# A two-layer trunk with 16 routed experts: fixed queue order in the experts, layer 1's first expert fed from on-chip rows, and the overflow branch moved

## The chip, the cores and the metric

One NeuronCore of one Trainium2 chip runs the whole program. The metric is the device time of one execution in microseconds (us).

## The reference

Two layers over 512 tokens of width 1024, batch 1, all in fp32. Each layer ends with the same grouped mixture of experts:

```python
for i in range(DEPTH):                                   # 2 layers
    z = x @ w_in                                         # mixer i: gMLP gating, or a short convolution
    tok, q = mixer(z), z[..., -512:]
    xa = memory_cross_attention(q, mem, w_kv[i])         # 256 memory rows
    o = concatenate([tok, xa]) @ w_out[i]
    x = layer_norm(ALPHA * x + o, ln1_g[i], ln1_b[i])
    scores = sigmoid(x @ router_w); sel = scores + router_b   # shared router, 16 experts
    # 1 of 4 groups by the sum of its top two, then the top two experts of that group
    for e in range(16):
        h = silu(x @ w_gate[i, e]) * (x @ w_up[i, e])    # 1024 -> 512
        f = f + combine[:, e] * (h @ w_down[i, e])       # 512 -> 1024
    x = layer_norm(ALPHA * x + f, ln2_g[i], ln2_b[i])
```

## The kernel before

**Products.** Every fp32 product is three fp32r products (`mm3`, L202 to L204): high by high, high by low, low by high. Weights come as 1 MB loads (`raw`, issued by SP, L147). ACT rounds each to its high part (L168) and DVE subtracts to get the low part (L169). Some splits of a 0.5 MB half (`split`) run their second step on POOL. Pages of 1 MB form a ring; a page comes free when the last reader is done, and with it a load may start.

**Mixer end** (`mixer_end`, `project_out`). The output projection makes columns 0 to 511 of all four row blocks first, then 512 to 1023 block by block (`oa`). After each block the rows are normalised (DVE), written to DRAM twice by POOL's queue (`x1d` to gather from, `rd` to add to), transposed (`rt`) and multiplied with the router (`lg`).

**Routing** (`route`, `entries`, `tables`, `overflow`). A chain of small DVE operations makes `oh` (token by expert, 0/1); products with `tri` and `ones_b` make each token's place in its expert's list (`pos`). `sel` blocks (128x128, 0/1) times `tok` make a table of token numbers and gates (`tab`, then `idxs` and `gates`); `cnt` and `nover` say whether an expert has more than 128 tokens.

**Experts** (`experts`). 16 experts, each on 128 slots: POOL gathers the rows of `x1d` into `xg`; PE transposes them (`xt`, 8 operations), ACT and DVE split them (`xgt`); PE does gate and up (`ga`, `ua`, 48 products of 512 columns), ACT Silu, DVE the product `h`, PE transposes `h` (`htr`, 4) and does down (`ya`, 24), ACT scales by the gate, POOL scatters with addition into `rd`. Expert e's down stands behind gate and up of e+1. Layer 0 fills the time until its first gather lands with keys and values of layer 1 (`fill0`: `ka`, `va`).

**Branch** (`more`, L889, L890). Every engine reads `nover` and skips a loop for overfull experts. It is skipped on these inputs, but no engine's later instructions start before it passes the branch, and it drains first. It stands behind expert 0's gate and up.

**Order.** A scheduler that simulates the program sets each engine's order, which is fixed in the program; only the tail after the last expert is written by hand.

Of the kernel before, what the change touches and what calls it, by code (L numbers as in the profile page):

```python
# [27 lines left out]
P = 128  # L28
# [7 lines left out]
E = 16  # L36
# [11 lines left out]
def trunk(ctx, tc, x, mem, w_in_a, sgu_ln_g, sgu_ln_b, sgu_w, sgu_b, w_in_b, conv_w, w_kv, w_out,  # L48
# [270 lines left out]
    def keys_values():  # L319
# [15 lines left out]
        for j in range(4):  # L335
            g = W.next()
            for kk in range(2):
                k = 2 * j + kk
                for m in range(2):
                    ms = slice(m * P, (m + 1) * P)  # L340
                    mm3(a[m], (memh[:, k, ms], meml[:, k, ms]), (g[:, 0, kk, :], g[:, 1, kk, :]),
                        k == 0, k == KB - 1)
            W.done(g)
        for m in range(2):
            split_to(vt[:, 0, m, :], vt[:, 1, m, :], a[m])
        return kt, vt
# [107 lines left out]
    def norm(r, stats, g, b, nd):  # L454
# [7 lines left out]
        vec.scalar_tensor_tensor(r, r, mv[:, 0:1], g, op0=OP.subtract, op1=OP.mult)  # L462
        rs = small.tile([P, 1], FT, name="rstd")
        vec.reciprocal(rs, sd)
        return vec.scalar_tensor_tensor(r, r, rs, b, op0=OP.mult, op1=OP.add)

    def project_out(i, ch, cl, lnp, after):
# [25 lines left out]
        for c in range(NC):  # L493
            o = acc("oa")
            for j in range(KB):
                mm3(o, lhs(order[j], c), (gs[j // 2][:, 0, j % 2, :], gs[j // 2][:, 1, j % 2, :]), j == 0, j == KB - 1)
                if c == NC - 1 and j % 2:
                    W.done(gs[j // 2])
            half(c, 1, o)
            if c % 2:  # L500
                drop(ch[c // 2], cl[c // 2])
            after(c, norm(xrow[c], st[c], lnp[:, 0], lnp[:, 1], D))
# [10 lines left out]
    def logits(c, i, lg):  # L513

        pool_e.dma_start(x1d[i][c * P:(c + 1) * P, :], xrow[c])
        pool_e.dma_start(rd[i][c * P:(c + 1) * P, :], xrow[c])
        xt = page("x1t", [P, KB, P])
        for q in range(2):
# [3 lines left out]
            act.activation(xt[:, 4 * q:4 * q + 4], t, AF.Copy)  # L522
        for k in range(KB):
# [3 lines left out]
    def route(c0, n, lg, after, rp):  # L527

        cs = slice(c0, c0 + n)

        at = [1280 if c0 else 0]

        def T(name, *shape):
            k = math.prod(shape)
            at[0] += k
            t = rp[:, at[0] - k:at[0]]
# [3 lines left out]
        def ranks(v, g, name):  # L540
# [4 lines left out]
            df, eq = T("df" + name, g, 4, 4), T("eq" + name, g, 4, 4)  # L545
# [5 lines left out]
            rk = T("rk" + name, g, 4)  # L551
# [3 lines left out]
        sc = T("sc", n, E)  # L555
        act.activation(sc, lg, AF.Sigmoid)
        sel = T("sel", n, E)
        with tc.issue_after(after.ins):
            vec.tensor_tensor(sel, sc, rb[:, None, :].to_broadcast([P, n, E]), op=OP.add)
        g4 = lambda a: a.rearrange("p n (g b) -> p (n g) b", g=G)  # L560
        rk = ranks(g4(sel), n * G, "e")
        top = T("top", n * G, 4)
        vec.scalar_tensor_tensor(top, rk, 2.0, g4(sel), op0=OP.is_lt, op1=OP.mult)
        gs = T("gs", n, G)
        vec.tensor_reduce(gs.rearrange("p n g -> p (n g)"), top, axis=AX.X, op=OP.add)
        gr = ranks(gs, n, "g").rearrange("p n g -> p (n g)")
        ing = T("ing", n * G)
        vec.tensor_scalar(ing, gr, 0.0, None, op0=OP.is_equal)
        ib = ing[:, :, None].to_broadcast([P, n * G, 4])
        vec.scalar_tensor_tensor(g4(oh[:, cs]), rk, 2.0, ib, op0=OP.is_lt, op1=OP.mult)  # L570
        oh2 = T("oh2", 2, n, E)
        for k in range(2):
            vec.scalar_tensor_tensor(g4(oh2[:, k]), rk, float(k), ib, op0=OP.is_equal, op1=OP.mult)
        entry = lambda j: tok[:, cs, :, :, j].rearrange("p c k e -> p k c e")
        vec.tensor_tensor(entry(0), oh2, row1[:, None, cs, None].to_broadcast([P, 2, n, E]), op=OP.mult)
        pos = bank([P, n, E], "pos")
        for c in range(c0, c0 + n):
            for j in range(c):
                pe.matmul(pos[:, c - c0], ones_b, oh[:, j], start=(j == 0), stop=False)
            pe.matmul(pos[:, c - c0], tri, oh[:, c], start=(c == 0), stop=True)  # L580
        os = T("os", n, E)
        vec.tensor_tensor(os, oh[:, cs], sc, op=OP.mult)
        vec.scalar_tensor_tensor(posp[:, cs, :], pos, 1.0, oh[:, cs], op0=OP.add, op1=OP.mult)
        pk = T("pk", 2, n, E)
        vec.tensor_tensor(pk, oh2, posp[:, None, cs, :].to_broadcast([P, 2, n, E]), op=OP.mult)
        vec.tensor_reduce(pos2[:, :, cs], pk, axis=AX.X, op=OP.add)
        den = T("den", n)
        vec.tensor_reduce(den, os, axis=AX.X, op=OP.add)
        rec = T("rec", n)
        vec.reciprocal(rec, den)  # L590
        vec.scalar_tensor_tensor(os, os, 1.0 / ALPHA, rec[:, :, None].to_broadcast([P, n, E]), op0=OP.mult, op1=OP.mult)
        gk = T("gk", 2, n, E)
        vec.tensor_tensor(gk, oh2, os[:, None].to_broadcast([P, 2, n, E]), op=OP.mult)
        vec.tensor_copy(entry(1), gk)
        vec.tensor_tensor(entry(2), gk, entry(1), op=OP.subtract)
        entries(range(c0, c0 + n))

    def overflow():

        cnt = tiny(E, "cnt")  # L600
# [10 lines left out]
    tab, last_entry = [], []  # L611
# [8 lines left out]
    def entries(cs):  # L620

        for c in cs:
            if c == 0:
                tab[:] = [tiny(3 * E, "tab")]
            for k in range(2):
                m = pe.matmul(tab[0], choose(pos2[:, k, c:c + 1]), tok[:, c, k].rearrange("p e t -> p (e t)"),
                              start=(c + k == 0), stop=(c + k == NC))
        last_entry.append(m.ins)

    def tables():  # L630

        t = tab[0].rearrange("p (e t) -> p e t", t=3)
        vec.tensor_scalar(idxs, t[:, :, 0], 1.0, None, op0=OP.subtract)
        return vec.tensor_reduce(gates, t[:, :, 1:3], axis=AX.X, op=OP.add)
# [15 lines left out]
    def experts(i, lnp, fill, after, stop, fine=False):  # L650
# [6 lines left out]
        xt = page("xgt", [P, 2, KB, P], FR)  # L657
# [21 lines left out]
        def gate_up(e, between=None):  # L679
            a = [acc("ga"), acc("ua")]  # L680
            for half in range(2):
                if half and between is not None:
                    between()
                for u in range(2):
                    for j in range(2):
                        g = W.next()
                        for kk in range(2):
                            k = 4 * half + 2 * j + kk
                            m = mm3(a[u], (xt[:, 0, k, :], xt[:, 1, k, :]), (g[:, 0, kk, :], g[:, 1, kk, :]),
                                    k == 0, k == KB - 1)  # L690
                        W.done(g)
            act.activation(hp[:, 0, :], a[0], AF.Silu)
            vec.tensor_tensor(hp[:, 1, :], hp[:, 0, :], a[1], op=OP.mult)
# [8 lines left out]
        def down(e, evict):  # L702
            for n in range(2):
                o = acc("ya")
                for j in range(2):
                    g = W.next()
                    for kk in range(2):
                        k = 2 * j + kk
                        mm3(o, (ht[:, 0, k, :], ht[:, 1, k, :]), (g[:, 0, kk, :], g[:, 1, kk, :]), k == 0, k == 3)
                    W.done(g)  # L710
                evict(n, o)
# [267 lines left out]
    kt, vt = keys_values()  # L979
# [56 lines left out]
    W.keep = 3  # L1036

    def mixer_end(i, ch, cl, lnp):
        lg = [tiny(3 * E, "lg"), None]

        def after(c, normed):
            if c == 0:
                W.on_pool = (lambda n: n % 2 == 1) if i == 0 else (lambda n: n % 3 != 0)
                W.keep, W.ahead = (2, 3) if i == 0 else (1, 2)
                W.pump()
            if c == NC - 1:
                lg[1] = bank([P, E], "lg3")
                lg.append(normed)
            logits(c, i, lg[1] if c == NC - 1 else lg[0][:, c * E:(c + 1) * E])
# [4 lines left out]
        project_out(i, ch, cl, lnp, after)  # L1054
        drop(lnp)
        rp = page("route", [P, 2048])
        route(0, 3, lg[0].rearrange("p (n e) -> p n e", e=E), lg[2], rp)
        route(3, 1, lg[1].rearrange("p (n e) -> p n e", e=E), lg[2], rp)
        tables()
        drop(rp)  # L1060
        overflow()
        W.ahead = 4

    mixer_end(0, ch, cl, lnp)
# [5 lines left out]
    def fill0():  # L1070
        kv1.append(keys_values())
        drop(memh, meml)
    xhl = []
# [6 lines left out]
    experts(0, (ln2_g[0], ln2_b[0]), fill0, next_x, stop)  # L1080
    kt, vt = kv1[0]
# [34 lines left out]
    W.keep = 3  # L1116
# [37 lines left out]
```

## Time and profile before

| what | us |
|---|---|
| time, median of 3 runs (lowest to highest) | 1063.36 (1061.95 to 1065.77) |
| the profiled execution | 1063.26 |
| its span | 1061.6 |
| PE busy in the span | 991.3 |
| DVE busy | 780.7 |
| ACT busy | 628.6 |

Busy time of PE is not time at full speed: it includes stretches at half clock. In rows of the trace, the first column is the start in us from the span's start, the second the duration; behind the shape stands "[idle before <- what ended it]".

### The profile page before, as it was taken

Reading aid. Unit: us, or ns where it says so; the run is one execution under the profiler, and the core shown is the slowest. Engines: PE = TensorE matmul, PEld = TensorE weight load, DVE = VectorE, ACT = ScalarE, POOL = GpSimd, SP = SyncE. Lnnn points to the kernel's source line nnn. Section 1 sums busy time; section 2 is a strip of 40 time slices with the busy share of each in tenths; the row PEclk is TensorE's granted clock in tenths of the full one; section 3 lists DMA queues with packets and bytes.
Section 4 is the critical chain, followed back from the end, with each engine's and each line's share of the span. In section 5 each row is a group of like instructions: output and inputs, shape, how many; then the busy total and the mean of one; then the engine's idle time right before and its main releaser. Section 6 shows DMA issues by size and latency. Waiting matters only on the chain. (4 is left out here: it accounts for less than half of the span.)

```text
span 1061.6 us, 12769 instructions
## 1 busy us (share of the span) xinstructions
PE 991.3 (93%) x4815; PEld 812.6 (77%) x4816; DVE 780.7 (74%) x880; ACT 628.6 (59%) x682; POOL 170.8 (16%) x115
## 2 busy tenths in 40 slices
PE   8999999769999999899899999986699999998995
PEld 6788889658888887678679887875588888886873
DVE  4638667866889976788794656475789999777885
ACT  4526533446788865767653514232688888767762
POOL 0000004311222212101101000212022222221123
PEclk9999999979999999999999999986899999999998
DMA  9713358568999999999690414492499999999934
GB/s 323 274 41 119 120 198 296 181 224 287 361 371 307 396 350 330 319 319 338 175 390 26 159 51 159 148 390 74 172 362 349 371 341 376 354 356 335 333 67 157
DMA packets 102220, 273.31 MB, mean 257 GB/s; under 512 B 10442, under 2 KB 10966, under 8 KB 102152
## 3 DMA queue, kind: packets, MB, share of 16 engines
q1 hardware_dynamic: 89480, 242.84, 62.8%
q0 software_dynamic: 11808, 26.97, 9.1%
q10 hardware_dynamic: 864, 2.62, 0.7%
q8 instruction: 39, 0.64, 0.2%
q14 instruction: 29, 0.24, 0.1%
HBM read 262.22 MB, written 26.21 MB: 272 GB/s over the span
## 5 line engine op out<-in xcount | busy, mean ns | idle before, releaser
L169 DVE TENSOR_TENSOR low<-raw,high 128x2048 fp32r<-128x2048 f32 x189 | 429.8, 2290 | 90.6 <-ACT high L168 87.2
L168 ACT ACTIVATE high<-raw 128x2048 fp32r<-128x2048 f32 x189 | 358.2, 1913 | 44.8 <-PE ga L204 33.4
L168 ACT ACTIVATE split<-raw 128x1024 fp32r<-128x1024 f32 x66 | 68.5, 1058 | 76.5 <-PE za L204 26.0
L203 PE MATMUL ua<-low,xgt 128*128 128x512 f32 x248 | 97.8, 394 | 9.0 <-DVE low L169 9.0
L202 PE MATMUL ya<-high,ht 128*128 128x512 f32 x256 | 103.5, 406 | 1.3 <-ACT high L168 1.3
L203 PE MATMUL ya<-low,ht 128*128 128x512 f32 x256 | 102.3, 400 | 2.1 <-DVE low L169 2.1
L204 PE MATMUL ya<-high,ht 128*128 128x512 f32 x256 | 101.8, 398 | 0.8 <-DVE ht L208 0.7
L203 PE MATMUL ga<-low,xgt 128*128 128x512 f32 x248 | 99.9, 403 | 2.1 <-DVE low L169 1.9
L202 PE MATMUL ga<-high,xgt 128*128 128x512 f32 x248 | 100.4, 405 | 0.0
L204 PE MATMUL ga<-high,xgt 128*128 128x512 f32 x248 | 98.1, 396 | 0.0
L169 DVE TENSOR_TENSOR split<-raw,split 128x1024 fp32r<-128x1024 f32 x57 | 68.7, 1221 | 39.7 <-ACT split L168 38.9
L202 PE MATMUL ua<-high,xgt 128*128 128x512 f32 x248 | 97.4, 393 | 0.1
L204 PE MATMUL ua<-high,xgt 128*128 128x512 f32 x248 | 96.9, 391 | 0.0
L667 POOL DMA_INDIRECT xg<-x1d,idxs x32 | 49.8, 1556 | 267.6 <-PE xt L676 238.3
L169 POOL TENSOR_TENSOR split<-raw,split 128x1024 fp32r<-128x1024 f32 x9 | 21.7, 2406 | 284.8 <-DVE sto L474 148.9
L207 ACT ACTIVATE xgt<-xt 128x512 fp32r<-128x512 f32 x64 | 36.4, 592 | 50.3 <-PE ua L203 26.0
L202 PE MATMUL za<-xh,split 128*128 128x512 f32 x160 | 61.9, 393 | 2.0 <-ACT xh L207 2.0
L203 PEld LDWEIGHTS ua<-low,xgt 128*128 128x128 f32 x248 | 46.6, 188 | 21.0 <-DVE low L169 11.7
L203 PE MATMUL za<-xl,split 128*128 128x512 f32 x160 | 62.5, 391 | 0.0
L204 PE MATMUL za<-xh,split 128*128 128x512 f32 x160 | 61.5, 390 | 0.0
L203 PEld LDWEIGHTS ya<-low,ht 128*128 128x128 f32 x256 | 48.6, 190 | 13.7 <-DVE low L169 3.1
L202 PEld LDWEIGHTS ya<-high,ht 128*128 128x128 f32 x256 | 48.6, 190 | 12.9 <-ACT high L168 1.8
(250 smaller groups left out, 1899.1 us busy)
## 6 DMA issues: line engine op xcount, KB each, us to landing
raw<-in_w_gate_dram SPq DMA_DIRECT2D x64, 1024.0 KB, 8.8
raw<-in_w_up_dram SPq DMA_DIRECT2D x64, 1024.0 KB, 8.3
raw<-in_w_down_dram SPq DMA_DIRECT2D x64, 1024.0 KB, 9.5
raw<-in_w_kv_dram SPq DMA_DIRECT2D x8, 1024.0 KB, 7.0
raw<-in_w_out_dram SPq DMA_DIRECT2D x8, 1024.0 KB, 6.1
raw<-in_w_in_b_dram SPq DMA_DIRECT2D x8, 1024.0 KB, 10.2
raw<-in_w_in_a_dram SPq DMA_DIRECT2D x6, 1024.0 KB, 5.5
x1d<-x POOLq DMA_DIRECT2D x8, 512.0 KB, 5.8
```

The costliest lines, as they stand in the source:

```text
L168: act.activation(high, src, AF.Copy)
L169: (pool_e if self.on_pool(self.count) else vec).tensor_tensor(low, src, high, op=OP.subtract)
L202: pe.matmul(o, a[0], b[0], start=start, stop=False)
L203: pe.matmul(o, a[0], b[1], start=False, stop=False)
L204: return pe.matmul(o, a[1], b[0], start=False, stop=stop)
L207: r = act.activation(hi, src, AF.Copy)
L667: pool_e.indirect_dma_start(out=xg[:, e % 2], out_offset=None, in_=x1d[i], in_offset=bass.IndirectOffsetOnAxis(ap=tabs[e][0], axis=0), bou ...
```

## The change

In both layers the experts' instructions on PE, ACT and DVE are put in the order in which the code lists them (the scheduler no longer chooses), up to expert 14. Per expert that is: gate and up of e, the next expert's transposes, down of e-1, the transposes of `h`. The product `h` and the scaling are issued ahead of the release of the last weights.

Layer 0: the list of token numbers is made and gathered from before the gates are worked out; `xg` is zeroed by ACT and not by POOL; the branch stands ahead of expert 0, behind `va`.

Layer 1: the mixer's end is written out by hand. Chunks 0 and 1 are routed between the projection's products. The first expert's rows don't come through DRAM: 0/1 blocks `sel0` times `xrow` give its transposed rows in PSUM (`rows0`, printed as `x`), fp32 products of 128 columns. The lists, gates and gathers of the other experts follow during expert 0. The branch stands behind gate and up of expert 2.

```diff
     def experts(...):
-        xg = page("xg", [P, 2, D])
-        pool_e.memset(xg, 0.0)
...
-        gather(0)
-        gather(1)
-        if i:
-            with tc.issue_after(last_entry[-1]):
-                keep_warm(8)
-        fill()
-        rest = page("more", [P, 4, FE])
-        W.keep, W.flight = 0, 4
+        begin(gather, (1, 2) if i else (0, 1))
+        end = fill()
+        if not i:
+            more(i, hy)
+        W.keep, W.flight = i, 4
...
-        xtrans(0)
-        gather(2)
+        if not i:
+            with tc.issue_after(end):
+                xtrans(0)
+            gather(2)
+        in_order()
         for e in range(E):
+            if e == last:
+                order.close()
             up = gate_up(e, ...)
+            if i and e == 2:
+                order.close()
+                rest = page("more", [P, 4, FE])
+                more(i, rest)
+                drop(rest)
+                W.keep = 0
+                in_order()
             if e + 1 < E:
                 xtrans(e + 1)
             if e + 3 < E:
                 gather(e + 3)
-            if e == 0:
-                more(i, rest)
-                drop(rest)
-                W.pump()
...
+    def mixer_end_dense(ch, cl, lnp):
+        W.keep, W.ahead = 7, 4
...
+        def first_rows(c, ks=range(KB)):
+            for k in ks:
+                k0 = 4 * P * (k // 4) + 2 * P * (k % 4 // 2) + k % 2
+                pe.matmul(rows0[k // 4][:, k % 4 * P:(k % 4 + 1) * P], xrow[c][:, k0:k0 + 2 * P - 1:2], sel0[:, c],
+                          start=(c == 0 and k % 4 == 0), stop=(c == NC - 1), skip_group_check=True)
+        with tc.manual_schedule(engines={ET.PE, ET.Activation, ET.DVE}):
...
+            o = column(3, (3, 7), part)
+            rows(3, o, False)
+            keep_rows(3, 1)
+            rows0 = [acc("x0") for _ in range(2)]
+            xts[2] = row_blocks(2)
+            first_rows(0)
...
+            route.choose(3, 1, None, third)
+            first_rows(2)
+            route.place(3, 1, route.count(3, 1))
+            choose_first(3)
+            first_rows(3)
+            xt, xg = slots()
...
+                split_to(xt[:, 0, 4 * q:4 * q + 4, :], xt[:, 1, 4 * q:4 * q + 4, :],
+                         rows0[q].rearrange("p (k s) -> p k s", s=P))
+            sels = chosen()
+        def begin(gather, es):
+            listed(sels)
+            for e in es:
+                gather(e)
+            route.gates()
+            weighed(sels)
+            overflow()
```

PE's rows at the start of layer 1's first expert, before: the products with `tok`, eight idle products (`warm`), the count, then the transposes of gathered rows.

```order
2977 L626 MATMUL tab<-tok,sel 128x48 x6
2978 L580 LDWEIGHTS tri
2979 L580 MATMUL pos<-oh,tri 128x16
2980 L626 MATMUL tab<-tok,sel 128x48 x2
...
3004 L602 MATMUL cnt<-oh,ones_b 128x16
3005 L676 MATMUL xt<-ident,xg_5890 128x128 x12
3006 L202 MATMUL ga<-split_5553,xgt_5893 128x512
```

Now, at the same place (x_5741 and x_5742 are the two banks of `rows0`; x_4263 and x_4264 are `xrow`):

```order
2973 L616 LDWEIGHTS tri
2974 L616 MATMUL pos<-oh,tri 128x16
2975 L650 LDWEIGHTS ones_b
2976 L650 MATMUL cnt<-oh,ones_b 128x16
2977 L1166 MATMUL x_5741<-sel_457_5514,x_4264 128x128 x4
2978 L1166 MATMUL x_5742<-sel_457_5514,x_4264 128x128 x4
2979 L202 MATMUL ga<-split_5500,xgt_5858 128x512
```

No table, gather or transpose stands between the last chunk's places and the first product. The same place on ACT, now, with what each row waits for (DMASW are POOL's transfers):

```order
434 L1106 ACTIVATE xg_5859<-ident 128x2048 [waits Activation_49]
435 L168 ACTIVATE high_5933<-raw_5106 128x2048 [waits DMAHW2_49,Activation_49]
436 L168 ACTIVATE high_5959<-raw_5183 128x2048 [waits DMASW5_49,DMASW6_49,DMASW4_49,DMAHW4_49,DMASW3_49,PE_49]
437 L207 ACTIVATE xgt_5858<-x_5741 128x512 [waits PE_49]
438 L207 ACTIVATE xgt_5858<-x_5742 128x512 [waits PE_49]
```

The split of the first expert's rows stands behind a rounding that waits for POOL's transfers.

ACT's rows for one expert late in layer 0 (expert 13), before: `xgt`'s two halves, Silu (`h<-ga`) and the scaling (`h<-ya`) stand wherever the scheduler put them among the roundings (`high`).

```order
272 L168 ACTIVATE high_3891<-raw_3663 128x2048
273 L207 ACTIVATE xgt_1693<-xt 128x512
274 L168 ACTIVATE high_3907<-raw_3701 128x2048
275 L692 ACTIVATE h_1692<-ga 128x512
276 L168 ACTIVATE high_3923<-raw_3721 128x2048
277 L207 ACTIVATE xgt_1693<-xt 128x512
278 L714 ACTIVATE h_1692<-ya,gates 128x512
279 L168 ACTIVATE high_3939<-raw_3752 128x2048
280 L168 ACTIVATE high_3972<-raw_3770 128x2048
281 L207 ACTIVATE ht<-htr 128x512
```

Now, for the same expert, and so for every one up to 14:

```order
271 L168 ACTIVATE high_3881<-raw_3655 128x2048
272 L168 ACTIVATE high_3897<-raw_3692 128x2048
273 L168 ACTIVATE high_3913<-raw_3712 128x2048
274 L748 ACTIVATE h_1625<-ga 128x512
275 L168 ACTIVATE high_3931<-raw_3742 128x2048
276 L207 ACTIVATE xgt_1622<-xt 128x512 x2
277 L770 ACTIVATE h_1625<-ya,gates 128x512
278 L168 ACTIVATE high_3963<-raw_3760 128x2048
279 L770 ACTIVATE h_1625<-ya,gates 128x512
280 L168 ACTIVATE high_3983<-raw_3778 128x2048
281 L207 ACTIVATE ht<-htr 128x512
```

Three roundings stand ahead of Silu, a fourth ahead of both halves of `xgt`; the other two stand behind one scaling each. On SP the branch's row stands, in layer 0, behind 4 loads fewer than before, and in layer 1 behind 11 more (18 loads of experts ahead of it before, 29 now).

## Rows read from the trace of the kernel before

**Rows 1.** The page, the span in 40 equal slices of 26.5 us: what the DMA engines moved, GB/s.

```profile
GB/s 323 274 41 119 120 198 296 181 224 287 361 371 307 396 350 330 319 319 338 175 390 26 159 51 159 148 390 74 172 362 349 371 341 376 354 356 335 333 67 157
```

**Rows 2.** Busy time by stage: start:end and length, busy us of PE, PEld (weight load), DVE, ACT, POOL, each with its count, then granted clock, DMA share, GB/s. In order: layer 0's late experts; layer 1's first expert with the branch; layer 1's experts 1 to 10, and 11 to 15.

```profile
414.00:533.00 119.00, 107.53 (x475) 83.44 (x474) 93.50 (x62) 81.87 (x69) 14.48 (x10) 0.99 0.88 293
...
733.40:755.00 21.60, 13.16 (x57) 10.22 (x56) 12.04 (x10) 14.31 (x11) 1.70 (x2) 0.90 0.08 21
755.00:940.00 185.00, 185.00 (x865) 153.41 (x863) 163.27 (x103) 145.94 (x121) 44.54 (x20) 0.99 0.99 355
940.00:1036.00 96.00, 92.34 (x423) 73.67 (x422) 76.49 (x52) 67.66 (x57) 14.35 (x9) 1.00 0.79 262
```

**Rows 3.** PE in order of time, the transposes of `h`, one row an expert: layer 0's experts 9 and 14, layer 1's 5, 10 and 14.

```profile
401.85 0.60 PE L699 MATMUL htr<-ident,h 128*128 128x128 f32 x4
...
501.56 0.60 PE L699 MATMUL htr<-ident,h 128*128 128x128 f32 x4
...
846.02 0.60 PE L699 MATMUL htr<-ident,h 128*128 128x128 f32 x4
...
935.62 0.60 PE L699 MATMUL htr<-ident,h 128*128 128x128 f32 x4
...
1009.56 0.60 PE L699 MATMUL htr<-ident,h 128*128 128x128 f32 x4
```

**Rows 4.** One stall in layer 0's late experts: ACT, then DVE, then PE in order of time; last the waits of ACT from 400 to 515 us (us in total, times, longest).

```profile
408.72 0.60 ACT L207 ACTIVATE xgt<-xt 128x512 fp32r<-128x512 f32 x1 [1.88 <-PE ua L203]
412.16 1.91 ACT L168 ACTIVATE high<-raw 128x2048 fp32r<-128x2048 f32 x1
...
414.10 2.29 DVE L169 TENSOR_TENSOR low<-raw,high 128x2048 fp32r<-128x2048 f32 x1 [3.94 <-ACT high L168]
...
416.45 0.55 PE L203 MATMUL ya<-low,ht 128*128 128x512 f32 x1 [1.83 <-DVE low L169]
...
ACT xgt L207 <- PE ua L203: 11.0, 7, 1.9
```

**Rows 5.** DMA by queue from 760 to 940 us (packets, MB, share of 16 engines; q1 carries the weight loads), and a window at the end of layer 1, columns as in rows 2.

```profile
q1 hardware_dynamic: 20160, 58.90, 88.5%
...
1010.00:1020.00 10.00, 10.00 (x48) 8.21 (x47) 9.67 (x7) 8.83 (x7) 2.06 (x1) 1.00 0.21 28
```

**Rows 6.** Layer 1, from the last projection product to the first expert: PE, DVE, ACT and POOL, each in order of time; then the median landing of `rd`'s writes and of the gathers (us, last column), and fp32 products of 128 columns on PE (two records a product).

```profile
703.60 0.39 PE L204 MATMUL oa<-split,cl 128*128 128x512 f32 x1
...
733.36 0.78 PE L202 MATMUL ga<-split,xgt 128*128 128x512 f32 x1
...
705.37 1.21 DVE L169 TENSOR_TENSOR split<-raw,split 128x1024 fp32r<-128x1024 f32 x1
...
716.00 4.26 DVE L617 TENSOR_SCALAR sel<-slot,pos 128x128 fp32r<-128x128 f32 x3
...
722.55 0.18 DVE L570 SCALAR_TENSOR_TENSOR oh<-route 128x16 bf16<-128x16 f32 x1
...
714.56 0.18 ACT L556 ACTIVATE route<-lg 128x16 f32<-128x16 f32 x1 [3.02 <-PE lg L524]
...
710.28 0.53 POOL L516 DMA_DIRECT2D rd<-x  x1
...
rd<-x POOLq DMA_DIRECT2D x2, 512.0 KB, 8.0
xg<-x1d,idxs POOLq DMA_INDIRECT x4, 4.0
...
125.10 1.05 PE L1029 MATMUL mx<-sgu,v 128*128 128x128 f32 x8
125.91 0.48 PE L203 MATMUL xa<-pt,vt 128*128 128x512 f32 x1
```

**Rows 7.** Layer 1's branch: PE, then DVE in order of time, and the window of half clock behind it (columns as in rows 2).

```profile
746.66 0.39 PE L203 MATMUL ua<-low,xgt 128*128 128x512 f32 x1
746.88 0.39 PE L204 MATMUL ua<-high,xgt 128*128 128x512 f32 x1
754.41 1.09 PE L699 MATMUL htr<-ident,h 128*128 128x128 f32 x4 [7.14 <-DVEq L890]
755.15 0.78 PE L202 MATMUL ga<-high,xgt 128*128 128x512 f32 x1
...
751.93 2.28 DVE L169 TENSOR_TENSOR low<-raw,high 128x2048 fp32r<-128x2048 f32 x1
...
751.30:758.10 6.80, 3.69 (x11) 3.14 (x12) 6.47 (x6) 2.05 (x2) 0.00 (x0) 0.50 0.33 119
```

**Rows 8.** Layer 0, from the end of `va` to expert 1, PE; then DVE beside it.

```profile
206.44 0.62 PE L204 MATMUL va<-split,meml 128*128 128x512 f32 x2
...
219.41 0.77 PE L202 MATMUL ga<-split,xgt 128*128 128x512 f32 x1
...
237.97 1.09 PE L699 MATMUL htr<-ident,h 128*128 128x128 f32 x4 [5.59 <-DVEq L890]
238.71 0.78 PE L202 MATMUL ga<-high,xgt 128*128 128x512 f32 x1
...
209.75 0.16 DVE L633 TENSOR_SCALAR idxs<-tab 128x16 int32<-128x16 f32 x1
...
213.14 0.68 DVE L208 TENSOR_TENSOR vt<-va,vt 128x512 fp32r<-128x512 f32 x1
```

More of the change, by code (lines that the diff above doesn't have):

```diff
@@ L498, in project_out, with rows @@
                     W.done(gs[j // 2])
+            return o
+        def rows(c, o, wide=True):
             half(c, 1, o)
@@ L501, in project_out @@
                 drop(ch[c // 2], cl[c // 2])
-            after(c, norm(xrow[c], st[c], lnp[:, 0], lnp[:, 1], D))
+            return norm(xrow[c], st[c], lnp[:, 0], lnp[:, 1], D, wide)
+        return column, rows
     posp = consts.tile([P, NC, E], FT, name="posp")
@@ L618, in choose, with chosen, listed, weighed @@
         return sel
[L620 to L624, printed above, removed]
+    def chosen():
+        sels = page("sels", [P, NC, 2, P], FR)
+        for c in range(NC):
             for k in range(2):
[L626 to L634, printed above, removed]
+                vec.tensor_scalar(sels[:, c, k], slot1, pos2[:, k, c:c + 1], None, op0=OP.is_equal)
+        return sels
+    def listed(sels):
+        t = tiny(E, "rows")
+        for c in range(NC):
+            for k in range(2):
+                pe.matmul(t, sels[:, c, k], tok[:, c, k, :, 0], start=(c + k == 0), stop=(c + k == NC))
+        vec.tensor_scalar(idxs, t, 1.0, None, op0=OP.subtract)
+    def weighed(sels):
+        t = tiny(2 * E, "gates").rearrange("p (e t) -> p e t", t=2)
+        for c in range(NC):
+            for k in range(2):
+                pe.matmul(t, sels[:, c, k], tok[:, c, k, :, 1:3], start=(c + k == 0), stop=(c + k == NC))
+        vec.tensor_reduce(gates, t, axis=AX.X, op=OP.add)
+        drop(sels)
     def table(pp, rhs):
@@ L647, in table, with experts @@
         return idx, gt
-    def experts(i, lnp, fill, after, stop, fine=False):
+    def experts(i, lnp, fill, after, stop, xt, xg, begin, fine=False):
         last = E - 1
-        xg = page("xg", [P, 2, D])
-        pool_e.memset(xg, 0.0)
         hy = page("h", [P, 4, FE])
         hp = hy[:, 0:2]
-        xt = page("xgt", [P, 2, KB, P], FR)
         ys = [hy[:, 2:4].rearrange("p a b -> p (a b)"), y1]
@@ L1035, in trunk, with slots, mixer_end @@
     lnp = ln_params(ln1_g[0], ln1_b[0])
[L1036 to L1041, printed above, removed]
+    W.keep = 5
+    def slots():
+        xt, xg = page("xgt", [P, 2, KB, P], FR), page("xg", [P, 2, D])
+        act.activation(xg.rearrange("p a (k n) -> p (a k) n", n=P), ident[:, None, :].to_broadcast([P, 2 * KB, P]),
+                       AF.Copy, scale=0.0)
+        return xt, xg
+    def mixer_end(ch, cl, lnp):
+        column, rows = project_out(ch, cl, lnp)
+        route = Router()
+        for c in range(NC):
+            normed = rows(c, column(c))
             if c == 0:
-                W.on_pool = (lambda n: n % 2 == 1) if i == 0 else (lambda n: n % 3 != 0)
-                W.keep, W.ahead = (2, 3) if i == 0 else (1, 2)
+                W.on_pool = lambda n: n % 2 == 1
+                W.keep, W.ahead = 2, 3
                 W.pump()
[L1046 to L1049, printed above, removed]
+            keep_rows(c, 0)
+            logits(row_blocks(c), route.of(c))
             if c % 2:
@@ L1053, in after @@
                 W.pump()
-        project_out(i, ch, cl, lnp, after)
         drop(lnp)
[L1056 to L1064, printed above, removed]
+        for c0, n in ((0, 3), (3, 1)):
+            route.choose(c0, n, normed)
+            route.place(c0, n, route.count(c0, n))
@@ new lines, in mixer_end, with split, choose_first, part @@
+        xt, xg = slots()
+        def begin(gather, es):
+            route.both()
+            route.places()
+            sels = chosen()
[5 more added lines that the diff above has]
+            overflow()
+        return xt, xg, begin
+    def mixer_end_dense(ch, cl, lnp):
+        column, rows = project_out(ch, cl, lnp)
+        W.keep, W.ahead = 7, 4
+        W.pump()
+        W.hold = True
+        route = Router()
+        sel0 = page("sel0", [P, NC, P])
+        ready = y1[:, 0:1]
+        xts = {}
+        def split():
+            if W.raw and len(W.ready) < 4 and free_pages:
+                W.split()
+        def choose_first(c):
+            vec.tensor_scalar(sel0[:, c], slot1, posp[:, c, 0:1], None, op0=OP.is_equal)
+        def first_rows(c, ks=range(KB)):
[4 more added lines that the diff above has]
+        with tc.manual_schedule(engines={ET.PE, ET.Activation, ET.DVE}):
+            rows(0, column(0))
+            keep_rows(0, 1)
+            split()
+            split()
+            rows(1, column(1))
+            keep_rows(1, 1)
+            xts[0] = row_blocks(0)
+            split()
+            split()
+            rows(2, column(2, (3,), lambda j: logits(xts[0], route.of(0))))
+            keep_rows(2, 1)
+            xts[1] = row_blocks(1)
+            pos = []
+            def part(j):
+                if j == 3:
+                    logits(xts[1], route.of(1))
+                    route.choose(0, 2)
+                    act.activation(ready, ident[:, 0:1], AF.Sqrt)
+                else:
+                    pos.append(route.count(0, 2))
+                    route.place(0, 2, pos[0])
+                    choose_first(0)
+                    choose_first(1)
+            o = column(3, (3, 7), part)
[4 more added lines that the diff above has]
+            first_rows(0)
+            logits(xts[2], route.of(2))
+            route.choose(2, 1)
+            xts[3] = row_blocks(3)
+            first_rows(1, range(4))
+            logits(xts[3], route.of(3))
+            first_rows(1, range(4, KB))
+            pos.append(route.count(2, 1))
+            def third():
+                route.place(2, 1, pos[1])
+                choose_first(2)
+            route.choose(3, 1, None, third)
[3 more added lines that the diff above has]
+            first_rows(3)
+            drop(lnp, *xs)
+            xt, xg = slots()
+            route.both()
+            route.places()
+            for q in range(2):
+                split_to(xt[:, 0, 4 * q:4 * q + 4, :], xt[:, 1, 4 * q:4 * q + 4, :],
+                         rows0[q].rearrange("p (k s) -> p k s", s=P))
+            sels = chosen()
+        drop(sel0)
+        def begin(gather, es):
+            listed(sels)
+            for e in es:
+                gather(e)
+            route.gates()
+            weighed(sels)
+            overflow()
+        return xt, xg, begin
@@ L1065, in trunk @@
+    rows = mixer_end(ch, cl, lnp)
     kv1 = []
```

180 lines of the change are left out of this document (109 added, 71 removed).

## Prediction

> **What bounds the kernel now.** Start with the table of busy time. PE is busy for 991 of 1061.6 us, so a gain has to come from the stretches in which PE waits or runs at half clock. Second, busy time by stage [rows 2]. From 755 to 940 us, layer 1's experts 1 to 10, PE is busy all the time at a granted clock of 0.99, DVE 163 of 185 us and ACT 146: PE sets the pace and DVE has a tenth to spare. Late in layer 0 (414 to 533) PE idles 119.0 - 107.5 = 11.5 us, late in layer 1 (940 to 1036) 3.7, and during layer 1's first expert (733.4 to 755) 21.6 - 13.2 = 8.4.
>
> Third, the experts' period, read where `h` is transposed [rows 3]. Layer 1 takes (935.62 - 846.02)/5 = 17.92 us an expert. That is PE's own work: 72 products 0.22 to 0.23 apart [rows 7] are 16.3, and 12 transposes the rest. Late in layer 0 it takes (501.56 - 401.85)/5 = 19.94, so 10 us are lost over five experts.
>
> Fourth, why [rows 4]. At 408.72 ACT's next instruction is a rounding of transposed rows (`xgt`) that waits for PE; behind it in ACT's queue stands a rounding of weights (412.16) whose page is in. DVE waits 3.94 us for that one, and PE 1.83 for DVE at 416.45. From 400 to 515 us ACT waits 11.0 us in 7 such places. The weights are there and the order on ACT is what is late.
>
> Fifth, is DMA the bound? From 760 to 940 us the weight queue moved 58.90 MB [rows 5]: 6.29 MB an expert (6 loads), so 19.2 us an expert, against PE's 17.92. PE lives on loads in hand; these lasted, since at 1010 the loads are over (28 GB/s from 1010 to 1020) while PE works until 1036.
>
> **Layer 1, start of the first expert.** Before: last projection product at 703.60, first `ga` at 733.36 [rows 6], so 29.8. Now, from the end of the projection T:
> - T itself is about 1.3 later, my estimate for PE waiting for the places of chunks 0 and 1 ahead of the last three projection products; a few small DVE operations of 0.2 each (as `oh`, 0.18) stand between.
> - The last chunk's normalisation loses the 1.21 us split that stood in it (705.37). Its scores came at 714.56, 11.0 after the last product; I take 9.5.
> - From the scores to `oh` of the last chunk took 722.55 - 714.56 = 8.0, of which 4.26 are three `sel` at 716.00. Without these 3.7 are left. Behind that stand a weight split of one `low` (2.28, as at 751.93 [rows 7]), the place and `sel0` (1): 7.0 together.
> - The last chunk's eight fp32 products: 0.81 us for four of `mx` [rows 6], so 1.6. Rounding of the first half (0.60, as `xgt` in [rows 4]) and its low part (0.7): about 1.2 until the first product.
> Sum 1.3 + 9.5 + 7.0 + 1.6 + 1.2 = 20.6, against 29.8: **9 us** earlier. ACT's row ahead of `xgt` waits for POOL's transfers. The last write of `rd` was issued at 710.28 and such a write lands after 8.0, so 718.3; a rounding of 1.91 behind it ends at 720.2, near T + 16.6, where the first half is due at about T + 19: hidden by 2 to 3 us. ACT's zeroing of `xg` (128x2048, like a rounding, 1.9) lies in the same slack.
>
> **Layer 1, first expert to second.** Before, `ga` to `ga`: 755.15 - 733.36 = 21.8 [rows 6, 7], with PE standing from 746.88 to 754.41 at the branch while DVE finishes a split begun at 751.93. Behind it the clock is 0.50 until 758.1: of 755.15 to 758.1, 2.95 us, half is lost, 1.5. Now there is no branch here: 48 products (10.9), 12 transposes (1.4), Silu and `h` ahead of `htr` (2), and a wait for the second expert's gather. Its table is made during gate and up, about 7 us in; `idxs`, issue (1) and landing (4.0 [rows 6]) bring it to about 13, 1.5 later than PE wants it. That is 16. Gain 21.8 + 1.5 - 16 = **7**.
>
> **The branch behind expert 2** costs PE what DVE has left when PE arrives: `h` and one `low`, 0.7 + 2.3, and some drain: 3.5, plus 1.5 of half clock: **-5**. Below, 3; above, the 7.5 that it cost before. What is late next: SP passes it too, and the ring refills late. 29 loads instead of 18 are ahead of it, 11 x 3.2 = 35 us of transfers that fill the time in which DMA was at a share of 0.08 (733.4 to 755, [rows 2]); so this bubble is covered.
>
> **Layer 0, start.** Before: last `va` 206.9, lists at 209.75, `ga` at 219.41, expert 1 at 238.71, with 5.59 us at the branch [rows 8]. Now PE's order puts the tables ahead of a quarter of `ka` and all of `va` (2.7 + 48 x 0.227 = 13.6 us of cover for the gather). I take the tables at 203 (6 us earlier: neither POOL's memset nor the gates are in the way), `va` done at 216.6, the branch 4 behind it (DVE's last `vt` row at 213.14 ended 6.9 behind `va` before), transposes and split 2.2: `ga` at 222.8. Expert 0 then takes 14.3: expert 1 at 237.1, against 238.71 + 1.5 of half clock. Gain **3**; between -1 and 7, as the tables come 4 us later or earlier.
>
> **Fixed order.** Worked through by hand for one expert: three roundings and splits, Silu, a fourth, `xgt` twice, and one behind each scaling. With 1.91 and 2.29 a page, each low part is done before PE wants it, by 0.6 to 1.0 us only. Layer 1 before shows 17.92 with DVE and ACT as full. So layer 0's late excess goes: 99.71 - 5 x 17.92 = **10**. Layer 1's late part: 73.94 - 4 x 17.92 = 2.3, and at most the 3.7 of idle: **2.5**. The last expert (not in the order) I leave as it is.
>
> **Sum.** 9 + 7 - 5 + 3 + 10 + 2.5 = 26.5; the profiled execution took 1063.26, in line with the median of 1063.36, so **about 1037 us**.
>
> **A rule on DMA.** The slices of 26.5 us show up to 396 GB/s [rows 1]. The Trainium skill (DMA: Bandwidth & Descriptors, Specifications) gives a core's share of HBM as about 358 GB/s. By that an expert's 6.29 MB would need 17.6 us and its rows' transfers some more, as an estimate, so that PE's 17.92 would have no reserve; the trace passes that figure, and the forecast goes by the 19.2 us of the rows.
>
> **Rivals.**
> - *DMA takes the order's gain back.* At 19.2 us a load-bound expert, 14 experts need 14 x 1.3 = 18 us of loads in hand. Layer 0 has 4 loads fewer ahead of the branch, 13 us, and PE wants the end 13 us sooner. For: the share of 0.88 even while PE idled. Against: in layer 1 the loads were over 26 us before PE's end. If it binds, the 10 of layer 0 shrink to 2: 1045.
> - *The starts don't come.* ACT's queue runs in order: if the writes of `x` land 8 us later because weight loads fill the engines, `xgt` waits and 9 becomes 1 or 2. The Trainium skill (PSUM — Partial Sum Buffer, Engine vs sequencer instructions) says that ScalarE's queue is strictly first in, first out, so such a row holds up all behind it; [rows 4] agree (3.94 us). The gather of expert 1 then comes late too: 1047.
> - *Slower: the fixed order stalls in every expert.* Margins of 0.6 to 1.0 a step are thin, and a late scaling holds two roundings. With 19.94 us, as late in layer 0, 28 experts cost: layer 0's first nine periods +2 each, 18, with the 10 not gained; layer 1 14 x 2 = 28 less its 2.5: 1063 - 14 (the starts) + 46 = 1095. It decides from a period of 18.9: 28 x 0.95 takes all of the 26.5 below.
> - *The order changes nothing.* The late stalls return elsewhere; only the starts stay: 1063 - 14 = 1049.
>
> **Numbers.** Forecast 0.50 (its own range 1028 to 1043), DMA 0.13, starts 0.14, order without effect 0.10, stalling order 0.09, and 0.04 for losses that just meet the gains. The range is 1023 (the upper bounds of the starts and 3 from each layer's last expert) to 1053; above lie 0.11, below 0.07. Less than 0.3% (3 us) is what a measurement can't tell from no change: faster 0.87, same 0.04, slower 0.09.
>
> **What would show it.** Right: first `ga` of layer 1 about 21 us behind the last projection product, the clock back before it; no wait at `htr` of expert 0; 3 to 5 us of wait behind expert 2; `htr` 17.9 to 18.1 apart all through, and no PE wait for `low` late in layer 0. Wrong: ACT waiting for a transfer (`raw`) in the experts (DMA); `xgt` of the first expert behind a wait for `rd` (starts); waits of PE for `low` in each expert (order).

## The result, and the profile after

The changed kernel takes 1037.78 us (median; 1037.21 to 1039.62); its ratio to the kernel before is 0.9746 (95% interval 0.9707 to 0.9785). The forecast was 1037. The sum was right; three of its terms were not, and their errors cancelled, which is luck.

Cut the span where the first `ga` starts and where the last expert's `h` is transposed, in each layer. Columns as in [rows 2]: layer 0's experts, then layer 1's mixer with its routing, then layer 1's experts. Before:

```profile
219.40:526.60 307.20, 290.88 (x1318) 235.77 (x1316) 244.61 (x158) 223.41 (x184) 53.96 (x30) 0.98 0.91 317
526.60:733.40 206.80, 192.18 (x1011) 159.83 (x1011) 130.00 (x260) 73.30 (x134) 20.04 (x18) 0.94 0.50 182
733.40:1031.20 297.80, 285.75 (x1318) 234.09 (x1317) 249.75 (x162) 227.24 (x187) 60.59 (x31) 0.99 0.86 303
```

After:

```profile
224.90:509.80 284.90, 283.13 (x1322) 233.50 (x1322) 244.10 (x160) 221.95 (x185) 78.17 (x31) 1.00 0.95 337
509.80:709.00 199.20, 191.43 (x1048) 160.18 (x1046) 131.97 (x262) 80.66 (x140) 8.54 (x11) 1.00 0.45 159
709.00:1007.40 298.40, 290.64 (x1342) 239.83 (x1342) 248.13 (x171) 222.45 (x185) 75.17 (x32) 0.97 0.92 323
```

Layer 0's start comes 5.5 us later, its experts are 22.3 shorter, the way to layer 1's first expert 7.6 shorter, layer 1's experts 0.6 longer; the tail behind gives 0.5. Together 24.3, the difference of the spans (1061.6 and 1037.3). (The last window reaches 0.35 us past that transpose, which comes at 1007.05; cut there, layer 1's experts are 0.2 longer and the tail gives 0.1.)

The period, beside [rows 3], PE in layer 0, experts 1, 14 and 15:

```profile
257.83 0.60 PE L754 MATMUL htr<-ident,h 128*128 128x128 f32 x4
...
490.67 0.60 PE L754 MATMUL htr<-ident,h 128*128 128x128 f32 x4
509.80 0.60 PE L754 MATMUL htr<-ident,h 128*128 128x128 f32 x4
```

(490.67 - 257.83)/13 = 17.91 us, and no PE wait for `low` is left: the late stall of [rows 4] has no row to answer it. PE's longest waits from 226 to 1007 us:

```profile
PE xt L729 <- DMA xg<-x1d,idxs: 4.1, 1, 4.1
PE xt L729 <- DVEq L956: 3.7, 1, 3.7
PE x L1166 <- DVE sel L1160: 3.4, 2, 2.6
PE ga L204 <- DVE xgt L208: 1.7, 1, 1.7
```

Layer 1's start, beside [rows 6] (PE, then DVE, then POOL; L672 makes the 0/1 blocks of the list, L680 the list, L720 gathers), and the gathers' median landing from 700 to 730 us:

```profile
706.42 2.87 PE L1166 MATMUL x<-sel,x 128*128 128x128 f32 x16 [2.58 <-DVE sel L1160]
708.95 0.77 PE L202 MATMUL ga<-split,xgt 128*128 128x512 f32 x1
...
717.06 0.95 PE L680 MATMUL rows<-tok,sels 128*128 128x16 f32 x8
...
726.92 1.95 PE L729 MATMUL xt<-ident,xg 128*128 128x128 f32 x8 [4.11 <-DMA xg<-x1d,idxs]
...
712.14 1.65 DVE L672 TENSOR_SCALAR sels<-slot,pos 128x128 fp32r<-128x128 f32 x8
...
716.27 2.29 DVE L169 TENSOR_TENSOR low<-raw,high 128x2048 fp32r<-128x2048 f32 x1 [0.27 <-ACT high L168]
718.48 0.17 DVE L681 TENSOR_SCALAR idxs<-rows 128x16 int32<-128x16 f32 x1
...
719.42 1.07 POOL L720 DMA_INDIRECT xg<-x1d,idxs  x1 [21.99 <-DVE idxs L681]
...
xg<-x1d,idxs POOLq DMA_INDIRECT x3, 7.2
```

The first product is there without a gather, but the list is late: its blocks are done at 713.8, PE's order has their products at 717.06, and `idxs` then stands another half us behind a weight split. The gather lands after 7.2 us, not 4.0. Behind expert 2 the branch costs 4 us of gap and then half clock (products 0.43 apart), beside [rows 7]:

```profile
763.11 1.95 PE L729 MATMUL xt<-ident,xg 128*128 128x128 f32 x8 [3.65 <-DVEq L956]
...
765.29 0.63 PE L203 MATMUL ya<-low,ht 128*128 128x512 f32 x1
765.72 0.63 PE L204 MATMUL ya<-high,ht 128*128 128x512 f32 x1
```

Layer 0's start, beside [rows 8], PE, then DVE ahead of the branch:

```profile
193.06 0.19 PE L616 MATMUL pos<-oh,tri 128*128 128x16 bf16 x1 [3.66 <-DVE oh L601]
...
195.34 1.85 PE L680 MATMUL rows<-tok,sels 128*128 128x16 f32 x8 [1.74 <-DVE sels L672]
...
202.63 1.22 PE L204 MATMUL ka<-memh,split 128*128 128x256 f32 x4 [1.30 <-POOL split L169]
...
223.07 1.95 PE L729 MATMUL xt<-ident,xg 128*128 128x128 f32 x8 [5.95 <-DVEq L956]
224.86 0.80 PE L202 MATMUL ga<-split,xgt 128*128 128x512 f32 x1
...
217.22 2.29 DVE L169 TENSOR_TENSOR low<-raw,high 128x2048 fp32r<-128x2048 f32 x1 [3.18 <-PEq L956]
219.43 0.68 DVE L208 TENSOR_TENSOR vt<-va,vt 128x512 fp32r<-128x512 f32 x1
220.03 2.28 DVE L169 TENSOR_TENSOR low<-raw,high 128x2048 fp32r<-128x2048 f32 x1
222.23 0.69 DVE L208 TENSOR_TENSOR vt<-va,vt 128x512 fp32r<-128x512 f32 x1
```

The list is early, but PE waits in order for the routing (3.66 and 1.74 us) and for a weight split on POOL (1.30) ahead of the last of `ka` and all of `va`, and then until DVE has done two splits and both `vt`.

### The profile page after: what moved, and what is told of

It reads as the page before. It is cut to its first block, busy times and chain, and to the rows that moved or that the text cites. A ratio compares the mean times of both kernels' runs of the same rounds, so it can differ in the third digit from the quotient of the medians.

```text
span 1037.3 us, 12851 instructions
## 1 busy us (share of the span) xinstructions
PE 988.6 (95%) x4879; PEld 818.7 (79%) x4880; DVE 771.0 (74%) x879; ACT 632.4 (61%) x689; POOL 193.7 (19%) x109
## 5 line engine op out<-in xcount | busy, mean ns | idle before, releaser
L720 POOL DMA_INDIRECT xg<-x1d,idxs x31 | 77.7, 2506 | 288.4 <-PE xt L729 256.4
L169 DVE TENSOR_TENSOR split<-raw,split 128x1024 fp32r<-128x1024 f32 x60 | 74.4, 1253 | 41.7 <-ACT split L168 40.8
L203 PE MATMUL ga<-low,xgt 128*128 128x512 f32 x248 | 97.5, 393 | 0.0
L204 PEld LDWEIGHTS ya<-high,ht 128*128 128x128 f32 x256 | 48.5, 189 | 13.0 <-DVE ht L208 1.3
L716 POOL DMA_INDIRECT rd<-h,idxs x16 | 40.4, 2523 | 93.7 <-ACT h L770 93.7
L202 PEld LDWEIGHTS ya<-high,ht 128*128 128x128 f32 x256 | 48.9, 191 | 10.7 <-ACT ht L207 0.6
L207 ACT ACTIVATE xgt<-xt 128x512 fp32r<-128x512 f32 x62 | 34.0, 596 | 37.0 <-PE xt L729 37.0
```

The source lines that it names most:

```text
L169: (pool_e if self.on_pool(self.count) else vec).tensor_tensor(low, src, high, op=OP.subtract)
L202: pe.matmul(o, a[0], b[0], start=start, stop=False)
L203: pe.matmul(o, a[0], b[1], start=False, stop=False)
L204: return pe.matmul(o, a[1], b[0], start=False, stop=stop)
L207: r = act.activation(hi, src, AF.Copy)
L716: added[e] = pool_e.indirect_dma_start(out=rd[i], out_offset=bass.IndirectOffsetOnAxis(ap=tabs[e][0], axis=0), in_=ys[e % 2], in_offset=No ...
```

## The experiments

Times are compared by their ratio to the kernel before, run on the same chip, since that kernel's median was 1062 to 1068 in the four comparisons. Its single runs spread from 1061 to 1069 us on one chip, so ratios of different comparisons can differ by some 0.5% (5 us) without a cause. Traces have an offset too: the first projection product of layer 0, ahead of all that was changed, comes at 128.16 in the kernel before and at 126.33 with the order alone. Differences of a few us are therefore read from stretches of the traces as well.

**The order alone, both ways.** Undone in the changed kernel (first), and alone in the kernel before (second). In both it is the order of PE, ACT and DVE together. The second also issues `h` and the scaling ahead of the release of the weights, as the change does; the first leaves that in.

```diff
-            order.enter_context(tc.manual_schedule(engines={ET.PE, ET.Activation, ET.DVE}))
+            pass
```

> The changed kernel with one thing undone: in the experts the scheduler chooses the order of PE, ACT and DVE again. Theory (the order alone removed the waits of PE for DVE): the waits late in the experts come back, h's transposes again 18 to 21 us apart in the last third of a layer, and the time rises by 10 (layer 0's late experts) to 18 us (with its last expert and layer 1), to 1048 to 1056. Rival (the waits went because the branch and the loads were moved): the time stays within 3 us of 1037.8.

Measured: 1055.89, ratio 0.9925 (0.9897 to 0.9952). Without the order 19 us of 27 are gone by the ratios (13.6 by the traces, 1050.9 against 1037.3). ACT again waits for PE with roundings behind it, and PE for DVE from 400 to 525 us:

```profile
406.39 0.60 ACT L207 ACTIVATE xgt<-xt 128x512 fp32r<-128x512 f32 x1 [3.01 <-PE ua L203]
406.88 1.91 ACT L168 ACTIVATE high<-raw 128x2048 fp32r<-128x2048 f32 x1
...
PE ua L203 <- DVE low L169: 5.4, 4, 1.8
```

> The kernel before with one thing of the change: the experts' fixed order on PE, ACT and DVE; starts, tables and branch as before. Theory: PE's late waits in both layers go, h's transposes 17.9 us apart from expert 2 on, 10 to 18 us faster than before: 1046 to 1054. Rival (the order needs the new starts, or stalls in each expert): no faster than 1060.

Measured: 1039.64, ratio 0.9789 (0.9748 to 0.9830), faster than either theory. In the trace expert 0's `h` comes at 230.68 and not 237.97, 1.8 of it the offset of the traces; 3.4 because expert 1's transposes no longer stand ahead of the first product, where PE waited 2.48 us for their gather; 2.1 because PE waits 3.45 and not 5.59 us at the branch. From there to expert 15's `h` layer 0 takes (this kernel, then the kernel before; columns as in [rows 2])

```profile
230.70:503.30 272.60, 272.60 (x1265) 225.15 (x1266) 234.18 (x152) 212.95 (x177) 74.30 (x29) 0.99 0.97 345
```

```profile
238.00:526.60 288.60, 277.88 (x1264) 225.21 (x1264) 233.67 (x151) 213.01 (x176) 52.29 (x29) 0.99 0.93 324
```

so 16 us less, with PE busy throughout and the DMA engines at 0.97. From there to layer 1's first `h` it takes 3.0 more, and from that to the last `h` 4.5 less. The other parts of the change add only 0.4% to the order, within the two intervals.

**Layer 1's first expert through DRAM.** `mixer_end` of layer 0 used in layer 1 too, gathers of experts 0 and 1 issued together. This also gives up the order written by hand and the routing between the projection's products, and keeps as many pages free of loads (`W.keep`) as before:

```diff
-        begin(gather, (1, 2) if i else (0, 1))
+        begin(gather, (0, 1))
...
-    W.keep = 6
-    rows = mixer_end_dense(ch, cl, lnp)
+    W.keep = 3
+    rows = mixer_end(ch, cl, lnp, 1)
```

> The changed kernel with layer 1's mixer end made as layer 0's: no 0/1 products, expert 0 gathered through DRAM as the others, two gathers issued together; the branch stays behind expert 2. Theory (the on-chip rows are worth their 8 to 9 us at the first product, but 4 of them are given back at the wait for expert 1's gather, which here lands beside the first): 1042 to 1049. Rival (the gather is waited for either way, so the on-chip rows are worth nothing): 1036 to 1041.

Measured: 1041.82, ratio 0.9801 (0.9763 to 0.9839): 6 us above the changed kernel by the ratios, which overlap; in the traces the stretch from layer 0's last `h` to layer 1's last is 498.2 against 497.2 us. So the on-chip rows, with the hand-written end that goes with them, are worth 1 to 6 us.

**The list earlier.**

```diff
+            sels = chosen()
             for q in range(2):
                 split_to(xt[:, 0, 4 * q:4 * q + 4, :], xt[:, 1, 4 * q:4 * q + 4, :],
                          rows0[q].rearrange("p (k s) -> p k s", s=P))
-            sels = chosen()
```

> The changed kernel with the eight 0/1 blocks of layer 1's lists made on DVE ahead of the first expert's split instead of behind it, so that lists and gather come some 6 us earlier. Theory (PE's 4.1 us wait for expert 1's rows is the late list): that wait goes, the first product comes 1 to 2 us later, in all 1034.5 to 1037. Rival (the gather is slow beside the loads, whenever it is issued): the wait stays above 2 us and the time is 1037.5 to 1040.

Measured: 1038.34, ratio 0.9766 (0.9730 to 0.9803). The gather is issued at 714.95, 4.5 us earlier, and the wait for it is gone, as the theory says; in its place PE waits for the split at the next product (the range of times was missed):

```profile
725.12 1.11 PE L729 MATMUL xt<-ident,xg 128*128 128x128 f32 x8
...
728.93 0.50 PE L204 MATMUL ga<-high,xgt 128*128 128x512 f32 x1 [1.67 <-DVE xgt L208]
```

The trace is 1.4 us shorter, the times show no difference.

**Layer 0's start as before.** `old_logits`, `old_route`, `entries`, `tables` of the kernel before for layer 0, its branch behind expert 0, as many pages kept free of loads (`W.keep`) at the mixer's end as before:

```diff
-        begin(gather, (1, 2) if i else (0, 1))
+        if i:
+            begin(gather, (1, 2))
+        else:
+            gather(0)
+            gather(1)
         end = fill()
         if not i:
-            more(i, hy)
+            rest = page("more", [P, 4, FE])
...
+            if not i and e == 0:
+                order.close()
+                more(i, rest)
...
-    W.keep = 5
+    W.keep = 3
```

> The changed kernel with all of layer 0's start undone (routing, tables, gathers, POOL's zeroing and the branch behind expert 0 as in the kernel before); the experts' order and all of layer 1's changes stay. Theory (layer 0's new start costs 6 us: PE stands in order behind the routing and at the branch): h of layer 0's expert 0 transposed at 230 to 232 instead of 237.6, all behind it 6 us earlier: 1030 to 1034. Rival (layer 0's start is neutral; the difference was the run): 1036 to 1040.

Measured: 1031.98, ratio 0.9667 (0.9622 to 0.9712), the theory: expert 0's `h` at 232.4 and not 237.6. Layer 0's part of the change was a loss of about 6 us (6.9 by the traces, 1030.4 against 1037.3; 4.7 of it stands at layer 0's last `h`, with an offset of 1.6 against it).

**Only layer 0's branch back.** `more(0)` behind expert 0, the new routing kept.

> The changed kernel with one thing undone: layer 0's branch back behind expert 0's gate and up, the new routing and tables kept. Theory (of the 6 us that layer 0's new start costs, the branch in front is the larger part: 5.95 us of wait against 3.7 behind expert 0, and the list is early): expert 0's h at 233 to 235, 1033 to 1036. Rival (the cost is PE's wait in order for places and lists ahead of va, 7 us in three gaps, and the branch costs the same at both places): 1037 to 1039.

Measured: 1043.17, ratio 0.9779 (0.9735 to 0.9824): slower than either theory said (3.9 us in the traces, 1041.2 against 1037.3; by the ratios the intervals overlap). Expert 0's `h` comes at 244.1 and not 237.6, 1.7 of it the offset of the traces. PE passes to the transposes at 218.81 without a branch, and then (PE, then ACT)

```profile
223.54 0.50 PE L202 MATMUL ga<-split,xgt 128*128 128x512 f32 x1 [3.62 <-ACT xgt L207]
226.50 0.79 PE L204 MATMUL ga<-split,xgt 128*128 128x512 f32 x1 [2.22 <-DVE xgt L208]
244.07 0.63 PE L754 MATMUL htr<-ident,h 128*128 128x128 f32 x4 [3.45 <-DVEq L962]
...
221.09 1.91 ACT L168 ACTIVATE high<-raw 128x2048 fp32r<-128x2048 f32 x1
222.89 1.09 ACT L207 ACTIVATE xgt<-xt 128x512 fp32r<-128x512 f32 x2
```

So the 5.95 us "at the branch" were mostly no price of the branch: two weight splits and `vt` stand ahead of `xgt` on ACT and DVE, and PE waits for these with or without it. The first product comes 4.6 us behind `va` instead of 7.7, but the wait of 2.22 and half clock behind it (0.50 from 226.5 to 231.5 us) give these 3 us back, and behind expert 0 PE stands 3.45 at the branch as well.

**Layer 1's branch behind expert 0.**

```diff
-            if i and e == 2:
+            if i and e == 0:
```

> The changed kernel with one thing undone: layer 1's branch behind expert 0's gate and up instead of expert 2's. Theory (the branch's wait and the wait for expert 1's gather are at the same place, so they would overlap, but PE waits for all of DVE and SP's loads stop as before): the 4.05 us gap behind expert 2 goes and the one behind expert 0 grows from 4.4 to 7 to 10: 1037 to 1041. Rival (moving the branch is where layer 1's gain lies): 1042 or more.

Measured: 1033.28, ratio 0.9684 (0.9639 to 0.9728), better than both expected. Behind expert 0 PE stands once, for the gather and not for the branch, and behind expert 2 not at all:

```profile
727.46 1.95 PE L729 MATMUL xt<-ident,xg 128*128 128x128 f32 x8 [4.50 <-DMA xg<-x1d,idxs]
```

The move to expert 2 thus cost some 6 us (5.7 in the traces, 1031.6 against 1037.3; by the ratios 6.6, where the ends of the intervals overlap): it took the branch out of a wait that hid it.

**Put together.** Layer 0's old start with the early blocks:

> Both steps that the runs so far point to, put together: layer 0's start as before the change, and in layer 1 the 0/1 blocks of the lists ahead of the first expert's split. If the two gains add: 6 and 2.7 us off the changed kernel, 1028 to 1032. If the early blocks are worth nothing by the clock: as the kernel with layer 0's old start alone, 1030 to 1034.

Measured: 1032.79, ratio 0.9678 (0.9634 to 0.9722): the blocks are worth nothing. Layer 0's old start with both branches behind expert 0:

> The kernel before with two things of the change: the experts' fixed order, and layer 1's first expert fed from on-chip rows; all of layer 0's start, and the branch in both layers behind expert 0, as before the change. Theory (the two gains of putting them back, 6 and 5 us, lie in different layers and add): 1025 to 1029. Rival (they don't add: the loads, stopped at both branches, end late and PE waits for them late in layer 1): 1030 or more.

Measured over five runs: **1027.14, ratio 0.9630 (0.9605 to 0.9656)**, the fastest of all; the two add, within the interval. It keeps the order and layer 1's hand-written mixer end with its `W.keep`, and nothing else of the change. Taking from it the on-chip rows, or the order:

> As the kernel with both branches put back, but layer 1's expert 0 is gathered through DRAM (the new routing, lists and both gathers kept). Theory (the on-chip rows are worth little, as expert 1's gather is waited for in their place, and the branch hides in that wait): 1 to 4 us more than that kernel, 1027 to 1032. Rival (the on-chip rows are worth the 9 us of the prediction): 1034 to 1038.

Measured: 1028.54, ratio 0.9655 (0.9622 to 0.9687): no difference beyond the interval. From layer 0's last `h` to layer 1's last the traces take 493.5 us, 491.1 with the on-chip rows, and 503.1 with the order alone. So what gains in layer 1 are mainly the new routing and lists, which both kernels have (some 10 us); the 0/1 products and the hand-written end add 2.4 in the trace and nothing that shows in the time.

> As the kernel with both branches put back, but the scheduler chooses the experts' order, so layer 1's start is the only thing of the change that is left. Theory (order and start add: the order is worth 18 to 22): 1045 to 1050, that is 13 to 18 us faster than before. Rival (the start has no effect of its own without the order): 1056 or more.

Measured: 1058.96, ratio 0.9930 (0.9909 to 0.9950): the rival. Layer 1's start without the order gives 0.7%, and the order on top of it 3.0%. By the same ratios the start on top of the order gives 1.6%. Late in layer 1 the scheduler's order is worse here than before (periods of 22.2 and 20.8 us in experts 12 and 13), so part of the start's gain is lost again; why it chose so was not looked into.

## Why the prediction was right, and where its terms were wrong

Of the forecast 26.5 us the traces show 24.2, in other shares (us):

| term | forecast | in the traces |
|---|---|---|
| layer 1, start of the first expert | 9 | 7.6 |
| layer 1, first to second expert | 7 | 1.4 |
| the branch behind expert 2 | -5 | -6.5 |
| layer 0, start (to expert 1's `h`) | 3 | 0.3 |
| fixed order | 12.5 | 21.4 (16.5 in layer 0, 4.9 in layer 1) |

- **What bounds the kernel, and why PE stalled: right in the main.** PE's pace, forecast at 17.92 us an expert, is now held (17.91) in all but the first and last experts and, in layer 1, the one with the branch; with the order alone undone the stalls are back. In the stall of [rows 4] a second ACT row stands ahead of the rounding and holds it longer than `xgt` does, Silu waiting for `ga` (below); the prediction did not name it. The runs fix the order of PE, ACT and DVE together, so that ACT's order alone would do it is argued from such rows and not shown.

```profile
411.66 0.60 ACT L692 ACTIVATE h<-ga 128x512 f32<-128x512 f32 x1 [2.35 <-PE ga L204]
```

- **Fixed order, 10 + 2.5: too small, 19 to 23 in the two runs on it alone (13.6 and, less the offset, 23 by the traces; 32 in the last).** The step that failed is "the last expert I leave as it is" (the range allowed 3 a layer for it). With the order alone, layer 0's stretch from expert 0's to expert 15's `h` lost 16 us, 10 of them up to expert 14 and 6 in the last period (25.1 to 19.1): before, PE idled 2.4 us there and made 11 products of `ya` more, work that the late stalls had pushed back. In layer 1 the order gives 4.5 and not 2.5, 2.1 of it in the last period. And it moved expert 1's transposes behind the first product: with layer 0's old start expert 0's `h` comes at 232.4 instead of 238.0, a gain of 5 to 6 us that the prediction put into no term.
- **Layer 0's start, +3: wrong, about 0, and a loss beside the order.** The first `ga` is at 224.9, not 222.8, against 219.4 before; expert 0 without a branch makes that up (expert 1's first product at 238.3 against 238.7), and a wait of 1.7 for `xgt` follows. The estimate took the tables at 203, `va` done at 216.6 and the branch 4 behind it; the list came at 197.3 and `va` was done at 217.1, as forecast, but PE then stood 5.95. Before, `va` was done at 209.1 and not at 206.9 (the row at 206.44 in [rows 8] is not the last; that one is below), so DVE's last `vt` ended 4.7 and not 6.9 behind it. `va` is thus 8 us later than before, with 7 us of waits in PE's order ahead of it. Putting the old start back gains 6 us.

```profile
208.71 0.39 PE L204 MATMUL va<-split,meml 128*128 128x512 f32 x1
```

- **Layer 1's start, 9: right by the sum (7.6 in the row above), wrong in what brings it.** From the last projection product (690.96) to the first `ga` it takes 18.0 and not 20.6 - 1.3 = 19.3, but that product comes 4.2 later, counted from layer 0's last `h`, and not 1.3: transposes and router products went ahead of it. The clock was forecast to be back before the first `ga` and was not: it is 0.50 from 708.9 to 710.9. With the on-chip rows replaced by two gathers 1 to 6 us are lost, 2.4 in the last pair of traces.
- **First to second expert, 7: wrong, 1.4.** The prediction let the gather land 4.0 after its issue, a row from a stretch in which the DMA engines were at a share of 0.08 to 0.3. Now the loads run beside it and it takes 7.2; and `idxs` came 9.5 us after the first `ga` and not 8, since PE's order had the list's products late. The rows were there 18 us in and not 13: 20.4 us from `ga` to `ga` (708.95 to 729.38), not 16.
- **The branch behind expert 2, -5: near, -6.5** (24.4 from `h` to `h` less 17.9). That it would have been hidden behind expert 0 was missed: the prediction compared it with the price before, not with what else PE waits for at that place now.
- **Rivals.** DMA never binds: from 226 to 1007 us no wait of PE or ACT for a load is in the trace, though the engines are busy 0.95 of layer 0's experts and 0.92 of layer 1's. The starts did come short, by 3 us in layer 0 and 7 in layer 1, though not by ACT waiting for the writes of `x`, and the order's surplus covered it. Stalls in each expert did not show (that rival's 1095 also left out the 2.5 that it names: 1092.5).
- The Trainium skill's figure of about 358 GB/s (DMA: Bandwidth & Descriptors, Specifications) is no ceiling here: nine of the slices after (1037.3/40 = 25.9 us each) are at 359 to 382 GB/s, though the mean over layer 0's experts is 337.

```profile
GB/s 321 290 42 122 102 142 260 226 228 290 338 361 347 343 380 360 365 355 358 275 372 2 162 82 121 1 293 282 313 275 359 382 308 379 355 365 352 356 103 163
```

## What to carry to other kernels

Where one engine has no slack and two others feed it in order, look first at which instruction of the feeders waits with ready work behind it: putting that order right was worth more than everything else here, and a faster start gained 0.7% without it against 1.6% with it. The branch cost PE here what DVE still had queued (3.65 us behind expert 2, where DVE's last row ends at 762.95), so it belongs where the path waits for something else anyway. Price a transfer from a row with the traffic that will run beside it, and when a total comes out right, test the terms: two parts of the change were losses of 6 us each, and putting them back gave 1027.

## What the runs showed of the hardware

A gather of 128 rows lands 4.0 us after its issue where the DMA engines are at a share of 0.08 to 0.3 ([rows 6], before), 7.2 us after it at 0.96 with weight loads (719.4 to 726.9 us), and 9.5 us after it in the experts (740 to 920 us, 0.95), the last in the row below. After PE's stand of 4 us at the branch the granted clock is 0.50, the lower of its two levels (1.2 GHz), from 763 to 768 us; it is the same behind the gather's wait (0.54 from 724 to 731.5).

```profile
xg<-x1d,idxs POOLq DMA_INDIRECT x10, 9.5
...
724.00:731.50 7.50, 4.58 (x17) 4.22 (x18) 3.19 (x5) 2.93 (x4) 0.99 (x1) 0.54 1.03 361
763.00:768.00 5.00, 4.89 (x16) 4.23 (x17) 1.38 (x2) 1.19 (x2) 1.03 (x1) 0.50 0.94 354
```
